# Memory attention and gates of the first layer spread over more projections; low weight parts taken from GpSimd to VectorE

## The chip, the cores and the metric

The kernel runs on one core of a Trainium2 chip. The core has five engines with a queue each, which meet only at semaphores: TensorE (PE; PEld is its weight load), VectorE (DVE), ScalarE (ACT), GpSimd (POOL) and SyncE (SP), which here only issues DMAs. The metric is the device time of one execution in microseconds (us), the median of several runs. A page and a trace of one profiled execution stand beside it.

## The reference, cut to what matters

The program is a two-layer trunk over 512 tokens of width 1024. The first layer mixes with an mLSTM (four heads of 256, chunk-wise) and a cross-attention to 256 memory tokens; the second layer uses latent attention and the same kind of memory attention. What the change touches is in the first layer:

```python
h = rmsnorm(x, norm_g)
qk, v, o, z, i_pre, f_pre, mq, mz = split_cols(h @ w_in, ...)
qk = silu(causal_conv(qk, conv_w, conv_b))            # 4 taps
...
lfc = log_sigmoid(f_pre); b = cumsum(lfc)             # gates: running sums and maxima
ht  = mlstm_chunkwise(q, k, v, i_pre, f_pre)
...
q  = rmsnorm(mq, q_gain)                              # memory attention, 4 heads of 128
p  = softmax(q @ mk.T * 128 ** -0.5)
y_mem = (p @ mv) * silu(mz)
return x + concatenate([y_m, y_mem]) @ w_out
```

All of it is float32 in and out.

## The kernel before, in words

Every float32 operand of a product is kept as two parts: a high part (`wh` of a weight, `hTh` of the activations), which ScalarE makes by a copy to a narrower format, and a low part (`wl`, `hTl`), the rest, which a subtraction makes (`split`, lines 130 and 131). A product is then three passes on TensorE: high by high, low by high (both line 162) and high by low (line 167). A weight block of 128 x 1024 numbers is loaded by SyncE into `wr` (two buffers), split into `wh` and `wl` (two buffers each) by `load`, and used in 24 matmuls. PSUM results are `acc` (four banks), `att` (two banks, attention) and `tp` (two banks, transposes).

The stages of the first layer in order: `mem_kv` and `x_prep`; `mem_proj`, which makes the memory queries and their gate and, by the way, the eight gate columns of the mLSTM; `gates`; then `a_qk(0)`, `a_v(0)`, `a_oz(0)`, the projections for the first mLSTM head, with `mem_attn` woven between them; then the other heads. `weave(main, side, plan)` takes a step of `main`, then as many steps of `side` as the plan has for it. `a_qk(0)` has 12 steps, three for each of its four weight blocks (24 matmuls each, then a convolution on VectorE, lines 611 to 616, in the one buffer `kl`). `mem_attn` has six steps: step i transposes the softmax of head i-1 (line 364), makes the scores of head i (two `att` tiles of 12 matmuls in all, a softmax on VectorE and ScalarE, lines 324 to 337) and the values of head i-2 (line 342 is their gate). `gates` computes on ScalarE and VectorE over 4 x 512 and 128 x 512 numbers, sends four rows of `m4` by a GpSimd DMA (line 584), and ends with two groups of transposes on TensorE (lines 589 and 594) that make `bcol` and `em`; `a_attn(0)`, the first mLSTM attention, is the first to read these.

The source's order isn't the final order. A scheduler that reckons with modelled times lines up each engine's instructions; each engine then runs its line strictly in order and waits where an operand or a buffer is not there.

`on_pool` is an iterator of 17 flags. `load` takes one flag for each weight block, and where it is true, the low part is made by GpSimd. The first nine blocks (those of `mem_proj`) are false, the next eight (four of `a_qk(0)`, four of `a_v(0)`) are true, and after them VectorE makes all.

Of the kernel before, what the change touches and what calls it, by code (L numbers as in the profile page):

```python
# [8 lines left out]
F32 = mybir.dt.float32  # L9
# [4 lines left out]
ALU = mybir.AluOpType  # L14
AX = mybir.AxisListType

P = 128
S = 512
# [22 lines left out]
def weave(main, side, plan=()):  # L41
    for i, _ in enumerate(main):
        for _ in range(plan[i] if i < len(plan) else 1):
            next(side, None)
    for _ in side:
        pass


def chain(*gens):
    for g in gens:  # L50
        yield from g


def drain(g):
    for _ in g:
        pass
# [3 lines left out]
def trunk(ctx: ExitStack, tc: tile.TileContext, pv_d, pos_d, x_d, memT_d, wmem_d, wg_d, wa_d, woa_d,  # L60
          wkva_d, wql_d, wb_d, wkvb_d, wqup_d, wob_d, out_d):
    nc = tc.nc
    V, A, G, PE = nc.vector, nc.scalar, nc.gpsimd, nc.tensor
# [17 lines left out]
    def st(shape, tag, bufs=1, dt=F32):  # L81
        return POOLS.get(tag, sp).tile(shape, dt, tag=tag, bufs=bufs, name=nm(tag))
# [9 lines left out]
    def s2(shape=(P, 512)):  # L92
        return st(list(shape), "s2", NS2)
# [7 lines left out]
    def tps(shape=(P, 512)):  # L101
        return pp.tile(list(shape), F32, tag="tp", bufs=2, name=nm("tp"))
# [22 lines left out]
        return pv[:, o:o + 1]  # L125


    def split(hi, lo, src, scale=None, eng=V):
        if scale is None:
            A.activation(hi, src, AF.Copy)  # L130
            eng.tensor_tensor(out=lo, in0=src, in1=hi.bitcast(F32), op=ALU.subtract)  # L131
        else:
            A.activation(hi, src, AF.Identity, scale=scale)  # L133
            V.scalar_tensor_tensor(out=lo, in0=src, scalar=scale, in1=hi.bitcast(F32),
                                   op0=ALU.mult, op1=ALU.subtract)

    on_pool = iter(())

    def load(src, nk, ncol, gain=None, pieces=1, raw=None):
        n = nk * ncol  # L140
        if raw is None:
            raw = wp.tile([P, 1024], F32, tag="wr", bufs=2, name=nm("wr"))
            nc.sync.dma_start(raw[:, :n], src)
        hi = wp.tile([P, 1024], F32R, tag="wh", bufs=2, name=nm("wh"))
        lo = wp.tile([P, 1024], F32R, tag="wl", bufs=2, name=nm("wl"))
        r3 = raw[:, :n].rearrange("p (k c) -> p k c", k=nk)
        if gain is not None:
            G.tensor_tensor(out=r3, in0=r3, in1=gain.unsqueeze(2).broadcast_to([P, nk, ncol]), op=ALU.mult)  # L148
        for i in range(pieces):
            ps_ = slice(i * n // pieces, (i + 1) * n // pieces)  # L150
            split(hi[:, ps_], lo[:, ps_], raw[:, ps_], eng=G if next(on_pool, False) else V)
        return (hi[:, :n].rearrange("p (k c) -> p k c", k=nk), lo[:, :n].rearrange("p (k c) -> p k c", k=nk))

    def prod(items, start, stop):
# [317 lines left out]
    def new_mkv():  # L472
# [4 lines left out]
                    in1=pv[:, _PV["mkg"]:_PV["mkg"] + 2], op=ALU.mult)  # L477
# [11 lines left out]
    mkT, mv = new_mkv()  # L489
    hT = (st([P, KT, S], "hTh", 1, F32R), st([P, KT, S], "hTl", 1, F32R))  # L490
    yT = (st([P, 12, S], "yTh", 1, F32R), st([P, 12, S], "yTl", 1, F32R))
# [55 lines left out]
    def gates():  # L547
        ps = tps([36, S])
        for t in range(NT):
            PE.transpose(ps[:, t * P:(t + 1) * P], gtk[:, t], ident)  # L550
        gw = st([36, 2, S], "s4", 2)
        fr = gw[32:36, 0]
        e = gw[32:36, 1]
        A.activation(fr, ps[32:36], AF.Identity, bias=pv[32:36, _PV["gb"]:_PV["gb"] + 1])
        A.activation(e, fr, AF.Abs)
        A.activation(e, e, AF.Exp, scale=-1.0)
        A.activation(e, e, AF.Ln, bias=one[32:36])
        lf = s2([4, S])
        V.scalar_tensor_tensor(out=lf, in0=fr, scalar=0.0, in1=e, op0=ALU.min, op1=ALU.subtract)
        ir = s2([4, S])  # L560
        A.activation(ir, ps[0:4], AF.Identity, bias=pv[0:4, _PV["gb"]:_PV["gb"] + 1])
        mask = s2([4, S])
        V.memset(mask, 1.0)
        V.memset(mask.rearrange("p (a b) -> p a b", a=NT)[:, :, 0:1], 0.0)
        b = s2([4, S])
        V.tensor_tensor_scan(b, mask, lf, 0.0, op0=ALU.mult, op1=ALU.add)
        R = s2([P, S])
        V.memset(R, 0.0)
        V.tensor_tensor(out=R[0:4], in0=ir, in1=b, op=ALU.subtract)
        b3 = b.rearrange("p (a b) -> p a b", a=NT)  # L570
        T = tiny([4, 3, 4])
        V.tensor_copy(T[:, 0], b3[:, :, P - 1])
        V.tensor_tensor(out=T[:, 1, 0:3], in0=T[:, 0, 0:3], in1=T[:, 0, 1:4], op=ALU.add)
        V.tensor_tensor(out=T[:, 2, 0:2], in0=T[:, 1, 0:2], in1=T[:, 0, 2:4], op=ALU.add)
        V.memset(mask, 0.0)
        V.tensor_copy(mask.rearrange("p (a b) -> p a b", a=NT)[:, 1:4, 0], T[:, 0, 0:3])
        V.tensor_tensor_scan(ir, mask, R[0:4], 0.0, op0=ALU.add, op1=ALU.max)
        R3 = R.rearrange("p (a b) -> p a b", a=NT)
        for k in range(1, 4):
            n = NT - k  # L580
            V.tensor_tensor(out=R3[32 * k:32 * k + 4, 0:n], in0=R3[0:4, 0:n],
                            in1=T[:, k - 1, 0:n].unsqueeze(2).broadcast_to([4, n, P]), op=ALU.add)
        for h in range(4):
            G.dma_start(m4[32 * h:32 * h + 1, :], ir[h:h + 1, :])
        V.scalar_tensor_tensor(out=lf, in0=b, scalar=-1.0, in1=ir, op0=ALU.mult, op1=ALU.subtract)
        V.tensor_scalar(lf, lf, 85.0, None, op0=ALU.min)
        tp = tps([P, NT, P])
        for c in range(NT):
            PE.transpose(tp[:, c], R[:, c * P:(c + 1) * P], ident)
        for k in range(4):  # L590
            V.tensor_copy(bcol[:, :, k], tp[:, :, 32 * k:32 * k + 4])
        tp = tps([P, NT, 4])
        for c in range(NT):
            PE.transpose(tp[:, c], lf[:, c * P:(c + 1) * P], ident[0:4, 0:4])
        A.activation(em, tp, AF.Exp)
# [3 lines left out]
    def a_qk(h):  # L599
        i0 = 4 + 20 * (h // 2) + 12 * (h % 2)  # L600
        r = 4 + 2 * (h % 2)
        for n, name in enumerate("qk"):
            heads[h][name] = st([P, 2, S], "qk", 4, F32R), yT[n][:, r:r + 2]
        for i in range(4):
            w = load(wa_d[i0 + i], KT, P)
            ps = acc()
            yield from proj_T(w, hT, ps)
            j = (8 if i >= 2 else 0) + 2 * h + i % 2
            tmp = st([P, 2, S], "kl")
            raw, u = tmp[:, 0], tmp[:, 1]  # L610
            A.activation(raw, ps, AF.Copy)
            V.tensor_scalar(u, raw, col("cw", 48 + j), col("cb", j), op0=ALU.mult, op1=ALU.add)
            for d in range(1, 4):
                V.scalar_tensor_tensor(out=u[:, d:], in0=raw[:, :S - d], scalar=col("cw", (3 - d) * 16 + j),  # L614
                                       in1=u[:, d:], op0=ALU.mult, op1=ALU.add)
            silu2(u, u, raw)
            hi, lo = heads[h]["qk"[i // 2]]
            split(hi[:, i % 2], lo[:, i % 2], u)
            yield
# [7 lines left out]
    def a_v(pr):  # L627
        vs = []
        for j in range(2):
            v = wide("v", 2, F32R), st([P, NT, 256], "u4", 5, F32R)  # L630
            G.memset(v[0][:, :, 256:258].bitcast(F32), 1.0)
            heads[2 * pr + j]["v"] = v
            vs.append(v)

        def evac(t, ps):
            for j in range(2):
                split(vs[j][0][:, t, 0:256], vs[j][1][:, t], ps[:, j * 256:(j + 1) * 256])

        yield from tok_proj(8 + 20 * pr, evac)

    def a_oz(h):
        gt = st([P, NT, 256], ("gt", "z4")[h % 2])
        heads[h]["g"] = gt

        def evac(t, ps):
            th = s2()
            A.activation(th, ps, AF.Tanh, scale=0.5)
            V.scalar_tensor_tensor(out=th[:, 256:], in0=th[:, 256:], scalar=1.0, in1=ps[:, 256:],
                                   op0=ALU.add, op1=ALU.mult)
            V.scalar_tensor_tensor(out=gt[:, t], in0=th[:, :256], scalar=1.0, in1=th[:, 256:],  # L650
                                   op0=ALU.add, op1=ALU.mult)

        yield from tok_proj(4 + 20 * (h // 2) + (8, 16)[h % 2], evac)
# [75 lines left out]
           (256, [(wa_d[c], 4 * c, 4) for c in range(2)])]  # L729
    wa_d = wa_d[2:]  # L730
    mu = []
    on_pool = iter((False,) * 9 + (True,) * 8)
    drain(mem_proj(wqa, wa_d, hT, None, (("u4", 5), ("qk", 4)), mu, gate_cols))
    gates()
    weave(chain(a_qk(0), a_v(0), a_oz(0)), mem_attn(mu, mkT, mv, yT), (1, 0) * 6)
    weave(chain(a_qk(1), a_oz(1)), a_attn(0))
    rope_tables()
    weave(chain(a_qk(2), a_v(1), a_oz(2)), a_attn(1))
# [11 lines left out]
    op = out_proj(woa_d, yT, a_done)  # L750
# [8 lines left out]
    mT, _ = load_memT(False)  # L759
# [377 lines left out]
```

## Time and profile before

| what | value |
|---|---|
| median of 3 runs | 787.78 us (786.49 to 788.13) |
| the profiled execution | 786.21 us, its span 784.4 us |
| busy share of the span | PE 97%, PEld 83%, DVE 64%, ACT 51%, POOL 26% |
| chain that ended last | PE 82%, DVE 11%, ACT 2%, POOL 1% |
| mean granted TensorE clock | 0.995 of full speed |

Read it so: TensorE is busy nearly all the time, and the chain of work that ended last is mostly TensorE. The span is 1.8 us shorter than the execution's own time, which has a launch and an end around it. The shares are means over very different stages, so the stretch that the change touches, some 82 to 156 us after the span's start, is looked at by itself.

### The profile page before, as it was taken

Reading aid. Unit: us, or ns where it says so; the run is one execution under the profiler, and the core shown is the slowest. Engines: PE = TensorE matmul, PEld = TensorE weight load, DVE = VectorE, ACT = ScalarE, POOL = GpSimd, SP = SyncE. Lnnn points to the kernel's source line nnn. Section 1 sums busy time; section 2 is a strip of 40 time slices with the busy share of each in tenths; the row PEclk is TensorE's granted clock in tenths of the full one; section 3 lists DMA queues with packets and bytes.
Section 4 is the critical chain, followed back from the end, with each engine's and each line's share of the span. In section 5 each row is a group of like instructions: output and inputs, shape, how many; then the busy total and the mean of one; then the engine's idle time right before and its main releaser. Section 6 shows DMA issues by size and latency. Waiting matters only on the chain.

```text
span 784.4 us, 11003 instructions
## 1 busy us (share of the span) xinstructions
PE 760.9 (97%) x3956; PEld 651.3 (83%) x3956; DVE 499.7 (64%) x970; ACT 400.7 (51%) x940; POOL 204.9 (26%) x294
## 2 busy tenths in 40 slices
PE   6999989999999999999999999999898999999997
PEld 5798877888888888888888888999787888888886
DVE  7753399837768836766434644586668787785432
ACT  4855645526455435536333647367656565644220
POOL 5311331201110101001001175250876361900000
PEclk9999999999999999999999999999999999999999
DMA  9322211223131223224444532211321111511141
GB/s 341 118 88 81 81 55 54 81 82 107 53 109 54 72 89 115 74 83 147 173 162 134 168 123 76 71 62 57 95 71 58 55 48 38 188 54 55 58 157 53
DMA packets 25190, 75.35 MB, mean 96 GB/s; under 512 B 2864, under 2 KB 3504, under 8 KB 25136
## 3 DMA queue, kind: packets, MB, share of 16 engines
q1 hardware_dynamic: 23568, 72.39, 27.6%
q10 hardware_dynamic: 1440, 2.25, 0.8%
q8 instruction: 31, 0.51, 0.3%
q14 instruction: 23, 0.19, 0.1%
q0 software_dynamic: 128, 0.01, 0.0%
HBM read 70.44 MB, written 4.19 MB: 95 GB/s over the span
## 4 chain that ended last, share of the span: by engine, by line
PE 82%; DVE 11%; ACT 2%; POOL 1%; issue 1%; DVEq 0%; ACTq 0%; POOLq 0%
PE acc L162 45%; PE acc L167 23%; PE att L162 3%; PE att L994 2%; PE att L167 2%; DVE wl L131 1%; PE tp L981 1%; DVE tiny L324 1%; PE tp L917 1%; DVE kl L614 1%; PE att L700 1%; PE att L701 1%; PE att L699 1%; ACT s L334 1%; POOL tiny L188 1%
## 5 line engine op out<-in xcount | busy, mean ns | idle before, releaser
L131 DVE TENSOR_TENSOR wl<-wr,wh 128x1024 fp32r<-128x1024 f32 (+5 forms) x109 | 130.3, 1195 | 152.6 <-ACT wh L130 131.2
L130 ACT ACTIVATE wh<-wr 128x1024 fp32r<-128x1024 f32 (+5 forms) x117 | 117.9, 1009 | 141.2 <-PE acc L162 114.3
L162 PE MATMUL acc<-wh,hTl 128*128 128x512 f32 (+4 forms) x352 | 123.6, 361 | 0.0
L162 PE MATMUL acc<-wh,hTh 128*128 128x512 f32 (+4 forms) x352 | 123.4, 363 | 0.2 <-ACT hTh L133 0.2
L162 PE MATMUL acc<-hTh,wh 128*128 128x512 f32 x256 | 102.4, 400 | 0.0
L162 PE MATMUL acc<-hTl,wh 128*128 128x512 f32 x256 | 101.1, 395 | 0.0
L167 PE MATMUL acc<-wl,hTh 128*128 128x512 f32 (+4 forms) x352 | 88.9, 359 | 0.0
L162 PE MATMUL acc<-wh,yTh 128*128 128x512 f32 x192 | 75.0, 394 | 0.0
L162 PE MATMUL acc<-wh,yTl 128*128 128x512 f32 x192 | 74.8, 390 | 0.0
L162 PEld LDWEIGHTS acc<-wh,hTh 128*128 128x128 f32 x352 | 65.2, 188 | 9.7 <-ACT hTh L133 0.7
L162 PEld LDWEIGHTS acc<-wh,hTl 128*128 128x128 f32 x352 | 65.5, 188 | 8.2
L167 PE MATMUL acc<-hTh,wl 128*128 128x512 f32 x256 | 69.7, 392 | 0.0
L167 PEld LDWEIGHTS acc<-wl,hTh 128*128 128x128 f32 x352 | 61.7, 188 | 8.8
L148 POOL TENSOR_TENSOR wr<-wr,pv 128x1024 f32<-128x1024 f32 (+2 forms) x24 | 42.7, 1783 | 88.9 <-DMA wr<-in_wb_dram 44.3
L162 PEld LDWEIGHTS acc<-hTl,wh 128*128 128x128 f32 x256 | 48.5, 190 | 9.2
L162 PEld LDWEIGHTS acc<-hTh,wh 128*128 128x128 f32 x256 | 48.6, 190 | 9.1
L167 PEld LDWEIGHTS acc<-hTh,wl 128*128 128x128 f32 x256 | 47.7, 188 | 9.8
L167 PE MATMUL acc<-wl,yTh 128*128 128x512 f32 x192 | 53.3, 389 | 0.0
L187 POOL TENSOR_SCALAR tiny<-tiny 128x2 f32<-128x2 f32 (+4 forms) x36 | 10.1, 280 | 165.1 <-ACT junk L192 52.3
L162 PE MATMUL acc<-wh,u 128*128 128x384 f32 (+1 forms) x160 | 39.0, 369 | 3.3 <-ACT junk L192 2.3
L167 PEld LDWEIGHTS acc<-wl,yTh 128*128 128x128 f32 x192 | 36.0, 188 | 7.4
L162 PEld LDWEIGHTS acc<-wh,yTh 128*128 128x128 f32 x192 | 36.1, 188 | 7.2
(286 smaller groups left out, 1496.7 us busy)
## 6 DMA issues: line engine op xcount, KB each, us to landing
wr<-in_wa_dram SPq DMA_DIRECT2D x46, 512.0 KB, 3.2
wr<-in_wb_dram SPq DMA_DIRECT2D x16, 512.0 KB, 3.5
wr<-in_woa_dram SPq DMA_DIRECT2D x12, 512.0 KB, 3.2
wr<-in_wob_dram SPq DMA_DIRECT2D x12, 512.0 KB, 3.2
wr<-in_wmem_dram SPq DMA_DIRECT2D x8, 512.0 KB, 3.4
yTh<-in_wmem_dram SPq DMA_DIRECT2D x6, 512.0 KB, 6.6
s<-in_memT_dram SPq DMA_DIRECT2D x8, 256.0 KB, 4.1
yTl<-in_x_dram SPq DMA_DIRECT2D x4, 512.0 KB, 9.0
```

Of the source, the lines that this page charges most:

```text
L130: A.activation(hi, src, AF.Copy)
L131: eng.tensor_tensor(out=lo, in0=src, in1=hi.bitcast(F32), op=ALU.subtract)
L148: G.tensor_tensor(out=r3, in0=r3, in1=gain.unsqueeze(2).broadcast_to([P, nk, ncol]), op=ALU.mult)
L162: PE.matmul(ps, x if lhs else w_[0], w_[0] if lhs else x, start=start and id(ps) not in seen, stop=False)
L167: PE.matmul(ps, a_[0] if lhs else w_[1], w_[1] if lhs else a_[0], start=False, stop=stop and left[id(ps)] == 0)
L187: G.tensor_scalar(t, ss, mul, add, op0=ALU.mult, op1=ALU.add)
L188: G.tensor_tensor(out=out, in0=t, in1=mhalf[:, :n], op=ALU.pow)
L324: V.tensor_reduce(mx[:, j:j + 1], ps, axis=AX.X, op=ALU.max)
L334: A.activation(out[j], ps, AF.Exp, bias=nb[:, j:j + 1], scale=rq[:, j:j + 1], accum_out=sm[:, j:j + 1])
L614: V.scalar_tensor_tensor(out=u[:, d:], in0=raw[:, :S - d], scalar=col("cw", (3 - d) * 16 + j), in1=u[:, d:], op0=ALU.mult, op1=ALU.add)
L699: PE.matmul(ps[:, :258], ph[:, blk(c, i)], v[0][:, c], start=c == 0, stop=False)
L994: PE.matmul(ps[:, i * P:(i + 1) * P], vt[:, c, h * P:(h + 1) * P], pTs[h][:, o:o + P], start=c == 0, stop=c == i)
```

## The change

Four edits. (1) `on_pool` is gone: all low weight parts are made by VectorE. (2) The plan of the first weave is `(1, 0, 0) * 6` in place of `(1, 0) * 6`: the six steps of `mem_attn` stand at the main steps 0, 3, 6, 9, 12 and 15 in place of 0, 2, 4, 6, 8 and 10, so the last two reach into `a_v(0)`. (3) `gates` is cut in two by a `yield`: its arithmetic stands where it did, and its transposes with what follows them come after the fourth step of `mem_attn`. (4) The gate arrays `R` and `lf`, which must now live longer, move from the shared `s2` buffers into the buffer `e`, which `a_attn(0)` uses later.

```diff
-    def split(hi, lo, src, scale=None, eng=V):
+    def split(hi, lo, src, scale=None):
         if scale is None:
             A.activation(hi, src, AF.Copy)
-            eng.tensor_tensor(out=lo, in0=src, in1=hi.bitcast(F32), op=ALU.subtract)
+            V.tensor_tensor(out=lo, in0=src, in1=hi.bitcast(F32), op=ALU.subtract)
...
-    on_pool = iter(())
...
-            split(hi[:, ps_], lo[:, ps_], raw[:, ps_], eng=G if next(on_pool, False) else V)
+            split(hi[:, ps_], lo[:, ps_], raw[:, ps_])
...
-        lf = s2([4, S])
+        keep = st([P, 1280], "e", 1)
+        R, lf = keep[:, 0:S], keep[0:4, S:2 * S]
...
-        R = s2([P, S])
...
         V.tensor_scalar(lf, lf, 85.0, None, op0=ALU.min)
+        yield
         tp = tps([P, NT, P])
...
-    on_pool = iter((False,) * 9 + (True,) * 8)
     drain(mem_proj(wqa, wa_d, hT, None, (("u4", 5), ("qk", 4)), mu, gate_cols))
-    gates()
-    weave(chain(a_qk(0), a_v(0), a_oz(0)), mem_attn(mu, mkT, mv, yT), (1, 0) * 6)
+    gc = gates()
+    next(gc)
+
+    def memory_and_gates():
+        for i, _ in enumerate(mem_attn(mu, mkT, mv, yT)):
+            if i == 3:
+                drain(gc)
+            yield
+
+    weave(chain(a_qk(0), a_v(0), a_oz(0)), memory_and_gates(), (1, 0, 0) * 6)
```

The orders of the two built programs are the same up to `mem_proj` (but for one memset of the buffer `e`, which goes to the very start) and from the last matmuls of `a_v(0)` on; SyncE's order is the same throughout. Between, they differ on four engines. In the changed kernel the line numbers from 137 on are one or two lower than before (326 becomes 324, 589 becomes 588).

GpSimd before, from the end of `mem_proj` to the broadcast of the first mLSTM attention (`wl` are low weight parts, `m_82` is `m4`):

```order
L188 TENSOR_TENSOR rq_472<-tiny_756,mhalf 128x16
L131 TENSOR_TENSOR wl_989<-wr_986,wh_988 128x1024
L131 TENSOR_TENSOR wl_1122<-wr_1119,wh_1121 128x1024
L131 TENSOR_TENSOR wl_1228<-wr_1225,wh_1227 128x1024
L584 DMA m_82_463<-s_163_943 1x16x32 x4
L131 TENSOR_TENSOR wl_1361<-wr_1358,wh_1360 128x1024
L131 TENSOR_TENSOR wl_1423<-wr_1420,wh_1422 128x1024
L131 TENSOR_TENSOR wl_1453<-wr_1450,wh_1452 128x1024
L631 MEMSET v_1410 128x4x2
L131 TENSOR_TENSOR wl_1483<-wr_1480,wh_1482 128x1024
L131 TENSOR_TENSOR wl_1513<-wr_1510,wh_1512 128x1024
L631 MEMSET v_1413 128x4x2
```

And GpSimd in the changed kernel, the same place:

```order
L186 TENSOR_TENSOR rq_472<-tiny_756,mhalf 128x16
L582 DMA m_82_463<-s_163_943 1x16x32 x4
L630 MEMSET v_1371 128x4x2
L630 MEMSET v_1374 128x4x2
L663 ISA
```

The eight subtractions are gone, and GpSimd has next to nothing left here. VectorE in the changed kernel, from the first gate instruction on (`e_941` holds `R` and `lf`; `tiny_996` are the maxima of the first softmax, `att_989` its scores):

```order
L558 SCALAR_TENSOR_TENSOR e_941<-s_161_936 4x512
L565 SCALAR_TENSOR_TENSOR s_165_948<-s_164_945,e_941 4x512
L567 TENSOR_TENSOR e_941<-s_163_943,s_165_948 4x512
L570 COPY tiny_952<-s_165_948 4x4
L573 MEMSET s_164_945 4x512
L322 TENSOR_REDUCE tiny_996<-att_989 128x1 x2
L131 TENSOR_TENSOR wl_1147<-wr_1144,wh_1146 128x1024
L571 TENSOR_TENSOR tiny_952<-tiny_952 4x3
L579 TENSOR_TENSOR e_941<-e_941,tiny_952 4x384
L611 TENSOR_SCALAR kl_1039<-kl_1039,pv 128x512
```

The third low weight part now stands among the gate's work; two more stand ahead of these rows and five behind them. TensorE before, where the gate's transposes stand (`tp_969` and `tp_978`) in the third block of `a_qk(0)`:

```order
L162 MATMUL acc_1231<-hTh_177,wh_1227 128x512
L589 MATMUL tp_969<-ident,s_166_950 128x128 x4
L162 MATMUL acc_1231<-hTl_178,wh_1227 128x512
L162 MATMUL acc_1231<-hTh_177,wh_1227 128x512
L162 MATMUL acc_1231<-hTl_178,wh_1227 128x512
L162 MATMUL acc_1231<-hTh_177,wh_1227 128x512
L162 MATMUL acc_1231<-hTl_178,wh_1227 128x512
L162 MATMUL acc_1231<-hTh_177,wh_1227 128x512
L162 MATMUL acc_1231<-hTl_178,wh_1227 128x512
L594 MATMUL tp_978<-ident,s_162_941 128x4 x4
```

TensorE in the changed kernel, where they stand now: behind the values of memory head 1 (`att_1323`) and ahead of those of head 2 (`att_1415`), in `a_v(0)`:

```order
L160 MATMUL att_1323<-z_208_1164,mv_175 128x512
L165 MATMUL att_1323<-s_207_1163,v_176 128x512 x2
L588 MATMUL tp_1334<-ident,e_941 128x128 x4
L593 MATMUL tp_1343<-ident,e_941 128x4 x4
L160 MATMUL att_1415<-s_228_1269,mv_175 128x512
L160 MATMUL att_1415<-gt_1270,mv_175 128x512
L160 MATMUL att_1415<-s_228_1269,mv_175 128x512
L160 MATMUL att_1415<-gt_1270,mv_175 128x512
L165 MATMUL att_1415<-s_228_1269,v_176 128x512 x2
L362 MATMUL tp_1401<-ident,s_235_1297 128x128 x2
```

They have moved back to behind the first blocks of `a_v(0)`, and the memory attention's last heads, which before lay in the second half of `a_qk(0)` and the start of `a_v(0)`, now lie in `a_v(0)` with few projection matmuls between them. VectorE's rows for this place in the changed kernel (`tiny_1295` and `tiny_1314` are the biases of the two softmaxes of head 3, `gt_1270` the low part of head 2's transposed softmax):

```order
L322 TENSOR_REDUCE tiny_1292<-att_1285 128x1 x2
L613 SCALAR_TENSOR_TENSOR kl_1240<-kl_1240,pv 128x510
L324 SCALAR_TENSOR_TENSOR tiny_1295<-tiny_1292,rq_472 128x2
L131 TENSOR_TENSOR yTl_180<-s_222_1224,yTh_179 128x512
L613 SCALAR_TENSOR_TENSOR kl_1240<-kl_1240,pv 128x509
L333 RECIPROCAL tiny_1298<-tiny_1298 128x2
L322 TENSOR_REDUCE tiny_1311<-att_1304 128x1
L335 TENSOR_SCALAR s_235_1297<-s_235_1297,tiny_1298 128x256 x2
L322 TENSOR_REDUCE tiny_1311<-att_1304 128x1
L131 TENSOR_TENSOR gt_1270<-tp_1271,s_228_1269 128x512
L131 TENSOR_TENSOR gt_1270<-tp_1278,s_228_1269 128x512
L324 SCALAR_TENSOR_TENSOR tiny_1314<-tiny_1311,rq_472 128x2
```

The rows of the last head's two softmaxes stand mixed with the third convolution of `a_qk(0)` (`kl_1240`), and the scores that they read (`att_1285`, `att_1304`) hold the two `att` banks until ScalarE has read them.

## Rows read from the trace of the kernel before

**Rows 1.** Windows: stretch; busy us (instructions) per engine; granted clock; DMA.
```profile
94.00:142.00 48.00, 43.48 (x216) 35.71 (x215) 45.77 (x101) 25.79 (x59) 12.54 (x10) 0.96 0.14 45
160.00:520.00 360.00, 360.00 (x1772) 305.09 (x1771) 213.19 (x383) 175.04 (x366) 66.08 (x86) 1.00 0.32 105
```

**Rows 2.** Waits of TensorE from 84 to 165: us, times, longest.
```profile
PE tp L594 <- DVE s L586: 2.3, 1, 2.3
PE att L162 <- ACT s L334: 1.8, 2, 1.4
PE tp L589 <- DVE s L581: 0.4, 1, 0.4
```

**Rows 3.** Windows around the fall of the granted clock.
```profile
109.60:111.40 1.80, 1.80 (x13) 1.68 (x14) 1.80 (x7) 0.86 (x3) 0.00 (x0) 1.00 0.83 282
111.50:114.80 3.30, 3.30 (x12) 2.61 (x10) 2.94 (x13) 2.81 (x8) 0.00 (x0) 0.50 0.04 10
```

**Rows 4.** Timeline of GpSimd, 80 to 150: start us, us, instruction [idle before].
```profile
82.14 2.41 POOL L131 TENSOR_TENSOR wl<-wr,wh 128x1024 fp32r<-128x1024 f32 x1 [11.95 <-ACT wh L130]
...
105.89 2.68 POOL L131 TENSOR_TENSOR wl<-wr,wh 128x1024 fp32r<-128x1024 f32 x1
...
141.87 5.33 POOL L131 TENSOR_TENSOR wl<-wr,wh 128x1024 fp32r<-128x1024 f32 x2 [10.29 <-ACT wh L130]
```

**Rows 5.** Timeline of VectorE, 60 to 165: long instructions.
```profile
96.66 1.75 DVE L572 COPY tiny<-s 4x4 f32<-4x4 f32 x1
...
106.25 2.33 DVE L326 SCALAR_TENSOR_TENSOR tiny<-tiny,rq 128x2 f32<-128x2 f32 x1
...
115.25 2.23 DVE L612 TENSOR_SCALAR kl<-kl,pv 128x512 f32<-128x512 f32 x1 [0.52 <-ACT kl L611]
...
124.91 2.48 DVE L131 TENSOR_TENSOR yTh<-kl,qk 128x512 fp32r<-128x512 f32 x1 [0.65 <-ACT qk L130]
...
141.40 3.55 DVE L614 SCALAR_TENSOR_TENSOR kl<-kl,pv 128x510 f32<-128x510 f32 x2
144.87 2.89 DVE L131 TENSOR_TENSOR yTl<-s,yTh 128x512 fp32r<-128x512 f32 x1
```

**Rows 6.** The same view: the same kinds of instruction at other moments.
```profile
100.15 0.15 DVE L576 COPY s<-tiny 4x3 f32<-4x3 f32 x1
100.22 0.53 DVE L612 TENSOR_SCALAR kl<-kl,pv 128x512 f32<-128x512 f32 x1
100.67 0.14 DVE L326 SCALAR_TENSOR_TENSOR tiny<-tiny,rq 128x2 f32<-128x2 f32 x1
...
112.65 0.69 DVE L131 TENSOR_TENSOR yTh<-kl,qk 128x512 fp32r<-128x512 f32 x1 [0.30 <-ACT qk L130]
...
130.29 1.52 DVE L614 SCALAR_TENSOR_TENSOR kl<-kl,pv 128x511 f32<-128x511 f32 x2
```

**Rows 7.** The same view: a weight's low part, a gated product, two ends of a stretch.
```profile
60.32 1.23 DVE L131 TENSOR_TENSOR wl<-wr,wh 128x1024 fp32r<-128x1024 f32 x1 [4.76 <-ACT wh L130]
...
82.58 0.69 DVE L206 SCALAR_TENSOR_TENSOR u<-s,acc 128x512 f32<-128x512 f32 x1 [3.20 <-ACT s L205]
...
93.60 0.68 DVE L559 SCALAR_TENSOR_TENSOR s<-s 4x512 f32<-4x512 f32 x1 [2.93 <-ACT s L557]
...
154.34 1.96 DVE L131 TENSOR_TENSOR u<-acc,v 128x256 fp32r<-128x256 f32 x5
```

**Rows 8.** Chain that ended last, 40 to 165: start us, us, what.
```profile
67.70 1.81 PE acc L162 x8
...
87.74 0.44 PE tp L314 x4
...
155.22 0.45 PE acc L167 x2
```

**Rows 9.** Timeline of ScalarE: gate input, one exponential of a softmax.
```profile
93.60 0.68 ACT L561 ACTIVATE s<-tp,pv 4x512 f32<-4x512 f32 x1
...
134.37 0.55 ACT L334 ACTIVATE s<-att,tiny,rq 128x256 f32<-128x256 f32 x1
```

## The prediction

> **What bounds the kernel now.** TensorE is busy for 97% of the span and makes most of the chain that ended last, so only what TensorE loses can be won. I read its waits in the stretch of the change first: three lines, 2.3, 1.8 and 0.4 us, 4.5 in all, and each names VectorE or a softmax behind it [rows 2]. Then the granted clock: behind the 2.3 us wait a stretch lies at 0.50, 1.2 of 2.4 GHz [rows 3]. The busy time of the longer stretch tells how long that lasted: its mean clock is 0.96 over 48 us [rows 1], 1.9 us lost at most; by the edges that I see between 111.4 and 114.8 it is 3.4 us at half speed, 1.7 us lost. So TensorE loses 4.5 + 1.7 = 6.2 us, and that is the most that the change can give here.
>
> Then who makes it wait. In those 48 us VectorE is busy for 45.77 [rows 1]; it is the bound of this stretch. But not all of that is work. Six instructions, two of them low parts of 128 x 512, take far longer than others of their kind [rows 5, 6]: 1.75 against 0.15, 2.33 against 0.14, 2.23 against 0.53, 2.48 against 0.69, 3.55 for two against 1.52, 2.89 against 0.69. The excess is 1.60 + 2.19 + 1.70 + 1.79 + 2.03 + 2.20 = 11.5 us. Each lies on a subtraction of GpSimd, of which there are eight in seven rows; the first, one from the middle and the last, a pair, are shown [rows 4]: the one of 105.89 ends at 108.57, the 0.14 us instruction that began at 106.25 ends at 108.58. Under the first, at 82.14, the gated product at 82.58 takes 0.69 as usual [rows 7]; it reads one operand in PSUM, the six stalled ones read only SBUF. So I take it that VectorE stands still while GpSimd subtracts. And the 2.3 us wait of TensorE is for a gate instruction that stood right behind the stall of 106.25.
>
> The Trainium skill says so as a rule (SBUF — State Buffer, "Who interferes with whom"): GpSimd and VectorE share a port pair under an exclusive lock, and a VectorE instruction with two SBUF inputs, or in a two-port mode, waits for the whole of a GpSimd one. By it all six stalls go with the eight instructions; the trace's ends agree, 108.57 and 108.58.
>
> **The change part by part.**
>
> *Low parts to VectorE.* It removes eight instructions from GpSimd, 2.4 to 2.7 us each, and adds eight to VectorE at 1.23 [rows 7]. Two of them stand ahead of the gates, where VectorE waits anyway (3.20 us idle ahead of one row [rows 7]), and cost nothing. Six lie in the stretch: 6 x 1.23 = 7.4 us. The stalls, 11.5, go. A low part now waits in VectorE's line in place of starting right behind ScalarE; TensorE needs it eight matmuls after the high part, and set against each other the two queues leave from 0.7 us up for each. That is cover, not gain; where VectorE slips by more than that, each microsecond is one of TensorE's.
>
> *Gates.* The gate chain starts later: its input transposes stand three matmuls further back, 3 x 0.23 = 0.7 us [rows 8], and on ScalarE an activation of 0.68 us [rows 9] now stands ahead of the rest of the chain: 1.4 us in all. So VectorE's first gate instruction comes at 95.0, not 93.60 [rows 7]. The transposes that made TensorE wait (2.3 and 0.4) stand over 20 us later, when their input is long there. Their readers, in the first mLSTM attention, come later still. GpSimd's DMA of `m4` has nothing ahead of it now; SyncE's order is the same, and its buffers come free at VectorE's pace. I price all of these at nothing.
>
> *VectorE's pace.* From the first gate instruction to the first low part of v (93.60 to 154.34 [rows 7]) it takes 60.7 us now. Then 60.7 - 11.5 + 7.4 = 56.6, from 95.0 to 151.6: 2.7 us earlier. That leaves out two memsets that move ahead of the stretch.
>
> *TensorE's pace.* The transposes ahead of `a_qk(0)` are through at 87.74 + 0.44 = 88.2, and `a_v(0)` ends at 155.22 + 0.45 = 155.7 [rows 8]; without its 6.2 us of losses that is 149.5. New waits have to be added. I set the two queues against each other at the place where the last memory heads stand close together in `a_v(0)`. TensorE reaches the values of head 1 after 138 matmuls of 512 columns at 1.81 / 8 = 0.226, 48 of 256 at half that, and 28 transposes at 0.11 [rows 8]: 31.2 + 5.4 + 3.1 = 39.7, at 127.9. They need the bank of the scores whose softmax bias (`tiny_1295`) is VectorE's 77th instruction from 95.0 on. Its mean, stalls taken off, is (45.77 - 7.3) / 101 = 0.38 [rows 1] (7.3 being the four stalls in that window): 73 x 0.38 + 4 x 1.23 = 32.7, at 127.7; with two exponentials of 0.55 [rows 9] 128.8. So TensorE waits 0.9 us. Six matmuls bring it to 130.2; the gate's transposes want a `tp` bank that VectorE frees eight instructions after the bias, at 130.7: 0.5. The values of head 2 want the next bank: bias two instructions on, 131.5, exponentials till 132.6, while TensorE is there at 131.3: 1.3. Together 2.7 us of new waits, and TensorE gains 6.2 - 2.7 = 3.5.
>
> The two paces give 2.7 and 3.5; I take 3.3, nearer to TensorE's, since the memsets are missing from the other. From 156 on both programs run in the same order and TensorE is busy for all of the 360 us from 160 to 520 [rows 1], so the gain stays. On the profiled execution: 786.21 - 3.3 = 782.9. The median is 787.78, 1.57 above it, and runs are compared by that: 787.78 - 3.3 = 784.5.
>
> **The rivals.**
>
> *A, new waits eat it.* The three new waits lie within 4 us. If they act as the old one of 2.3 us did, the clock falls once more and 1.7 us go [rows 3]; and if VectorE slips by one more microsecond, that comes on top. For it: VectorE has no idle left up to there. Against: the 1.4 us wait [rows 2] was followed by no fall, since one fall alone makes the mean of 0.96 [rows 1]. Gain 0.6 to 1.6: 786.2 to 787.2, 786.7 in the middle.
>
> The Trainium skill (TensorE: Matmul & The Clock Gate, "Part 1: The HAM clock gate") has the clock set by how busy the engine has been of late, so several short waits may count as one; no row here shows it.
>
> *B, no new waits.* VectorE runs with fewer gaps than its mean [rows 1], and all 6.2 us are won: 787.78 - 6.2 = 781.6. Against: VectorE would have to be faster than 151.6 by 2 us.
>
> *C, slower: VectorE takes the whole load.* The place is the same stretch. If the six long instructions are not held by GpSimd but by something that stays (their own operands, or fetching of instructions), VectorE has 60.7 + 7.4 = 68.1 us of work from 95.0 on and ends at 163.1, 8.7 later; TensorE, which was 1.3 us behind it, follows some 7 us later: 795. It decides as soon as more than a quarter of the 11.5 us stays (2.7 / 11.5). Against: six stalls on six subtractions, and equal ends.
>
> The Trainium skill has the advice that speaks for C (Perfetto Trace Analysis, "Optimizing Scalar/DVE Operations"): where VectorE is saturated, work may go to GpSimd, and this change takes it back; the same paragraph warns of the shared port, and the six long rows bear the warning out [rows 5].
>
> **How the numbers follow.** The forecast, 784.5 (783 to 786), has 0.63; A 0.19; B 0.11; C 0.07. What a measurement of this kernel can tell from no change is about 0.2%, 1.6 us: faster means below 786.2. The forecast's and B's cases are faster, but for 0.01: 0.73. A counts as the same but for its worst, 0.18 with that 0.01; slower is C and A's worst, 0.09. The range reaches from just past B to past the middle of A, 781.4 to 787.4, and leaves out C and the rest of A.
>
> **What would show it.** Right: no VectorE instruction of these kinds over 1 us in the stretch but the scans and low parts, GpSimd without a subtraction, TensorE's waits there under 3.5 us, none of them for the gate's last instruction, no stretch at half clock, and `a_v(0)` ending some 3 us earlier. Wrong: the long instructions stay (C); a new line in TensorE's waits for `wl` on VectorE, or the clock at 0.5 near 130 (A). A gain at 156 that isn't there at the end would refute that the later order carries it.

## The result, and the profile after

The changed kernel took 781.34 us (780.85 to 782.65, 4 runs) against 787.81 (786.49 to 788.13, 4 runs): a ratio of 0.9924 [0.9906, 0.9941], 6.5 us less. In a second comparison (e7 below) it took 783.41 (781.83 to 785.10, 6 runs) against 787.37: 0.9956 [0.9941, 0.997], 4.0 us less. The ten runs of both have a median of 782.4, and 56 runs of the kernel before, over all comparisons, one of 786.9. The forecast of 784.5 had the sign and the mechanism. The second median lies in the 783 to 786 of its main case; the first lies outside that, by 1.66, and just outside the whole range of 781.4 to 787.4, by 0.06. Which of 3.3, 4.0 and 6.5 is the change's own, the traces tell better than the times, as shown below: it is 4.6.

The windows of the changed kernel that answer to [rows 1] (stretch, then busy us and instructions of PE, PEld, DVE, ACT, POOL; granted clock; DMA):

```profile
94.00:142.00 48.00, 46.07 (x238) 38.44 (x238) 46.79 (x108) 28.52 (x62) 2.41 (x5) 1.00 0.15 48
160.00:520.00 360.00, 360.00 (x1777) 305.65 (x1776) 217.98 (x391) 178.50 (x375) 69.72 (x97) 1.00 0.32 104
```

In the same 48 us TensorE ran 238 matmuls in place of 216, the clock did not fall, GpSimd's 12.54 us became 2.41 (the DMA of `m4` and a memset), and VectorE is as busy as before, but now with work. TensorE's waits from 84 to 165 us, for [rows 2]:

```profile
PE att L160 <- ACT s L332: 1.5, 2, 0.8
PE tp L588 <- DVE gt L131: 0.4, 1, 0.4
```

4.5 us have become 1.94. Where they lie, by TensorE's timeline (start us, us, instruction, [idle before <- releaser]):

```profile
128.93 0.50 PE L160 MATMUL att<-s,mv 128*128 128x512 f32 x1 [0.69 <-ACT s L332]
...
131.00 0.63 PE L588 MATMUL tp<-ident,e 128*128 128x128 f32 x4 [0.41 <-DVE gt L131]
...
132.81 0.50 PE L160 MATMUL att<-s,mv 128*128 128x512 f32 x1 [0.84 <-ACT s L332]
```

These are the three places that the forecast named. VectorE's timeline for [rows 5, 7]: the gate's start, the instruction that took 1.75, a weight's low part and the row behind it, the two biases of the forecast, the first low part of v:

```profile
94.64 0.68 DVE L558 SCALAR_TENSOR_TENSOR e<-s 4x512 f32<-4x512 f32 x1 [2.93 <-ACT s L555]
...
97.20 0.15 DVE L570 COPY tiny<-s 4x4 f32<-4x4 f32 x1
...
98.42 1.20 DVE L131 TENSOR_TENSOR wl<-wr,wh 128x1024 fp32r<-128x1024 f32 x1
99.55 0.14 DVE L571 TENSOR_TENSOR tiny<-tiny 4x3 f32<-4x3 f32 x1
...
127.48 0.15 DVE L324 SCALAR_TENSOR_TENSOR tiny<-tiny,rq 128x2 f32<-128x2 f32 x1
...
131.36 0.15 DVE L324 SCALAR_TENSOR_TENSOR tiny<-tiny,rq 128x2 f32<-128x2 f32 x1
...
147.61 0.42 DVE L131 TENSOR_TENSOR u<-acc,v 128x256 fp32r<-128x256 f32 x1
```

No single instruction in the stretch takes over 1.23 us; the longest are the weights' low parts and the scans. The chain of waits (start us, us, what) puts the end of `a_v(0)` at 150.37 + 0.45, against 155.67 in [rows 8]:

```profile
150.37 0.45 PE acc L165 x2
```

**A length that the rest of the execution can't blur.** Executions of one kernel spread by 2 to 4 us, more than some parts of the change are worth. But the stretch that the change touches has two ends that are the same work in all these kernels: the transposes ahead of `a_qk(0)` (TensorE, line 314 before, 312 after) and a memset of `v` by GpSimd near 200 us. The kernel before, and then the changed one:

```profile
87.58 0.60 PE L314 MATMUL tp<-ident,s 128*128 128x128 f32 x4
...
202.12 0.11 POOL L631 MEMSET v<- 128x8 f32 x1 [19.98 <-PE att L700]
```

```profile
87.36 0.60 PE L312 MATMUL tp<-ident,s 128*128 128x128 f32 x4
...
197.29 0.11 POOL L630 MEMSET v<- 128x8 f32 x1 [19.67 <-PE att L699]
```

202.12 - 87.58 = 114.54 us before, and in two more profiles of that kernel (e9, e10) 114.54 and 114.49. After the change it is 197.29 - 87.36 = 109.93 us, and in e7 109.93 again. So the change takes 4.6 us off its own stretch. Every kernel below was measured by these two rows; but for the two kernels named, each has one profile. The third column is half of the time at half clock:

| kernel | stretch, us | lost to half clock within, us | ratio of the times |
|---|---|---|---|
| before (three profiles) | 114.54, 114.54, 114.49 | 1.7, 1.7, 0 | 1 |
| changed (two profiles) | 109.93, 109.93 | 0, 0 | 0.9924 and 0.9956 |
| e1 low parts alone | 111.24 | 0 | 0.9965 [0.9951, 0.9979] |
| e2 spread and split alone | 114.38 | 1.7 | 1.0 [0.999, 1.0011] |
| e11 split alone | 114.15 | 3.4 | 0.9998 [0.9987, 1.0009] |
| e6 all but the spread (the same program, see there) | 109.89 | 0 | 0.9947 [0.9935, 0.9959] |
| e5 spread wider | 111.53 | 1.7 | 0.9957 [0.9946, 0.9969] |
| e12 gates later, no spread | 110.71 | 0 | 0.9958 [0.9943, 0.9973] |
| e8 two low parts on GpSimd | 110.38 | 0 | 0.9963 [0.9948, 0.9978] |
| e4 dummy memsets | 112.13 | 0 | 0.9983 [0.9971, 0.9996] |
| e3 dummy subtractions | 117.47 | 1.7 | 1.0043 [1.0029, 1.0057] |

### The profile page after: what moved, and what is told of

It reads as the page before. It is cut to its first block, busy times and chain, and to the rows that moved or that the text cites. A ratio compares the mean times of both kernels' runs of the same rounds, so it can differ in the third digit from the quotient of the medians.

```text
span 779.1 us, 11004 instructions
## 1 busy us (share of the span) xinstructions
PE 760.0 (98%) x3956; PEld 651.6 (84%) x3956; DVE 497.6 (64%) x978; ACT 401.7 (52%) x940; POOL 185.1 (24%) x286
## 4 chain that ended last, share of the span: by engine, by line
PE 82%; DVE 11%; ACT 2%; issue 1%; POOL 1%; DVEq 0%; ACTq 0%; POOLq 0%
PE acc L160 45%; PE acc L165 23%; PE att L160 3%; PE att L1000 2%; PE att L165 2%; DVE wl L131 2%; PE tp L987 1%; DVE tiny L322 1%; DVE kl L613 1%; PE tp L923 1%; DVE s L335 1%; PE att L699 1%; PE att L700 1%; PE att L698 1%; DVE s L910 1%
## 5 line engine op out<-in xcount | busy, mean ns | idle before, releaser
L131 DVE TENSOR_TENSOR wl<-wr,wh 128x1024 fp32r<-128x1024 f32 (+5 forms) x117 | 140.5, 1202 | 156.8 <-ACT wh L130 132.6
```

The costliest lines, as they stand in the source:

```text
L131: V.tensor_tensor(out=lo, in0=src, in1=hi.bitcast(F32), op=ALU.subtract)
```

## The experiments

Theory L is the forecast's: GpSimd's subtractions hold VectorE, and TensorE waits for what is held.

**e1: the low parts alone**, in the kernel before:

```diff
-    on_pool = iter((False,) * 9 + (True,) * 8)
```

> The kernel before with one edit: all low weight parts on VectorE, the spread of the memory attention and the gates as before. Theory L (VectorE stands still while GpSimd subtracts, and that is what TensorE waited for): the six stalls, 11.5 us, are gone against 7.4 us of added subtractions; TensorE's 2.3 us wait for the last gate instruction falls below 0.5 and the half clock behind it goes, the 1.8 us for the softmaxes may stay: a gain of 3 to 5 us, 783 to 785. Rival S (the gain comes from the wider spread and the later gate transposes, VectorE being saturated either way): within 1.5 us of before, 786.3 to 789.

784.21 us against 786.58, 2.4 less, stretch 111.24. All long VectorE instructions are gone, the waits for the gate too, without the gate having been touched. TensorE's waits:

```profile
PE att L162 <- ACT s L334: 1.5, 2, 1.3
PE att L162 <- ACT s L130: 0.6, 1, 0.6
```

3.3 of the 4.6 us of the stretch come from this one line.

**e2: spread, split gates and the buffer `e`**, the eight low parts still on GpSimd (the changed kernel with the `on_pool` lines put back).

> The changed kernel, but the eight low parts go to GpSimd as before: the spread and the later gate transposes alone. Theory L: the stalls stay, some 11 us, so VectorE stays the bound; TensorE loses its wait for the gates but waits longer for the last memory heads: gain 0 to 2.5 us, 785.3 to 788. Rival S: most of the gain of 6.5 us, 781.5 to 783.5.

786.74 against 786.58: nothing. TensorE's waits:

```profile
PE tp L364 <- DVE s L337: 2.9, 1, 2.9
PE acc L162 <- ACT kl L612: 0.9, 1, 0.9
PE att L162 <- ACT s L334: 0.6, 1, 0.6
```

The 2.3 us wait for the gate is gone and 2.9 us for the first softmax have come in its place: another instruction stands behind the same stall, as VectorE's timeline shows.

```profile
105.88 2.29 DVE L326 SCALAR_TENSOR_TENSOR tiny<-tiny,rq 128x2 f32<-128x2 f32 x1
...
108.44 0.60 DVE L337 TENSOR_SCALAR s<-s,tiny 128x256 f32<-128x256 f32 x2
```

**e3: the stalls put back without the work.** The changed kernel, VectorE making all low parts, and GpSimd doing eight subtractions of the same size that nobody reads:

```diff
+        if next(on_pool, False):
+            spare = tabs.rearrange("p a b c -> p (a b c)")
+            G.tensor_tensor(out=spare, in0=hi.bitcast(F32), in1=hi.bitcast(F32), op=ALU.subtract)
```

> The changed kernel, and beside it GpSimd does eight subtractions of 128x1024 that nobody reads, released by the same high weight parts as the real ones were, into a table that is only written later; VectorE, TensorE, ScalarE and SyncE have the changed kernel's order, instruction for instruction. Theory L: at least five VectorE instructions that read SBUF alone take 1.5 to 2.5 us more, four of them ahead of 129 us, so TensorE's waits there grow from 1.9 by 5 to 7: 786 to 790. Rival S, or stalls with another cause: no VectorE instruction is longer and the time is the changed kernel's, 781 to 782.5.

790.27 against 786.58, slower than the kernel before and just above the 786 to 790 expected by Theory L; the stretch is 7.5 us longer than the changed kernel's, though the other engines' instructions and their order are the same. VectorE's timeline has the long rows again, on other instructions than before, and one of GpSimd's is long itself:

```profile
97.53 2.20 DVE L572 TENSOR_TENSOR e<-s,s 4x512 f32<-4x512 f32 x1
...
107.60 3.35 DVE L588 SCALAR_TENSOR_TENSOR e<-s,s 4x512 f32<-4x512 f32 x1
```

```profile
96.77 2.42 POOL L154 TENSOR_TENSOR tabs<-wh 128x1024 f32<-128x1024 f32 x1 [5.07 <-ACT wh L130]
...
115.00 4.09 POOL L154 TENSOR_TENSOR tabs<-wh 128x1024 f32<-128x1024 f32 x1 [4.60 <-ACT wh L130]
```

This is the case that rival C feared, VectorE with both the low parts and the stalls, though by another cause; against the kernel before it costs 3.7 us, half of C's 7. TensorE waits 4.0 us for `wl` here, the line that the forecast had named for the case that VectorE falls behind.

**e4: GpSimd busy, but reading next to nothing.** In place of each dummy subtraction one of two columns and two memsets of the whole buffer:

```diff
+            G.tensor_tensor(out=spare[:, :2], in0=hi[:, :2].bitcast(F32), in1=hi[:, :2].bitcast(F32), op=ALU.subtract)
+            G.memset(spare, 0.0)
+            G.memset(spare, 0.0)
```

> As the kernel with eight idle subtractions, but GpSimd only writes: a subtraction of two columns, then two memsets of 128x1024 in its place. The other four engines have the changed kernel's order. If VectorE is held only where both want the second read path, two-input instructions go on and at most some one-input ones (copy, tensor_scalar) are held: 781 to 783.5, fewer than three long instructions. If any GpSimd work holds it, as with the subtractions: 785 to 790.

785.62 against 786.58: the time is at the lower end of the second expectation, while the instructions behave nearly as the first one says. GpSimd works nearly as long for each block (the memsets take 0.95 us each), but the stretch is 2.2 us longer than the changed kernel's, not 7.5. VectorE's rows, and GpSimd's memsets under them:

```profile
96.82 0.68 DVE L574 TENSOR_TENSOR e<-s,s 4x512 f32<-4x512 f32 x1
...
107.85 1.37 DVE L342 TENSOR_SCALAR s<-s,tiny 128x256 f32<-128x256 f32 x2
109.15 1.25 DVE L591 TENSOR_SCALAR e<-e 4x512 f32<-4x512 f32 x1
...
111.71 1.18 DVE L342 TENSOR_SCALAR s<-s,tiny 128x256 f32<-128x256 f32 x2
```

```profile
96.84 0.95 POOL L155 MEMSET tabs<- 128x1024 f32 x1
...
108.03 1.05 POOL L155 MEMSET tabs<- 128x1024 f32 x1
109.14 0.98 POOL L156 MEMSET tabs<- 128x1024 f32 x1
...
111.52 0.98 POOL L156 MEMSET tabs<- 128x1024 f32 x1
```

So it isn't GpSimd's being busy that costs most, it is its reading beside VectorE's reading. The Trainium skill (SBUF — State Buffer, "Who interferes with whom") says the same: a VectorE instruction with two SBUF inputs contends with a GpSimd one that reads SBUF, not with one that only writes it. The trace agrees: the two-input subtraction at 96.82 takes its usual 0.68 us under a memset. The 2.2 us that remain are most likely the three `TENSOR_SCALAR` rows above, which have one full-size input: they take 1.37, 1.25 and 1.18 where the changed kernel has 0.60, 0.41 and 0.60, 2.2 us more in all, and each lies on a memset. No run tests that by itself.

**e7: the changed kernel again**, on the chip of e5, e6 and e8.

> The changed kernel once more, nothing edited, as the measure for the three beside it. Both theories: 5 to 6.5 us under the kernel before, 780 to 782, TensorE's waits from 84 to 165 us near 1.9 in three lines. If the gain comes out under 4 us, part of the 6.5 of the first comparison was the spread of single runs.

4.0 us less, and 783.41 lies outside the expected 780 to 782; the waits are the same to the tenth (1.5 and 0.4). So part of the first 6.5 was the spread of single runs. In this profile the clock fell at 8 and at 551 us, in the first one near 588, and in both at the very end; the ones at 8, 551 and 588 last 3.4 us each and so take up to 1.7. The mean granted clock of the first comparison's four runs was 0.995 to 0.998, that of these six 0.992 to 0.997, which points to luck of this kind.

**e6: the old density**, plan `(1, 0) * 6`, low parts on VectorE and split gates kept.

> The changed kernel with the memory attention at its old density, plan (1, 0) * 6; low parts on VectorE and the split gates stay. The first study of parts gave 2.4 us for the low parts alone and nothing for spread and split gates alone, so 2 to 3 us come only from both. Theory P (the spread gives them: the heads stand two steps apart and TensorE waits for softmaxes): 2 to 3 us slower than the changed kernel, waits for att on ScalarE's s from 1.5 us up. Rival G (the gates' later transposes give them): within 1 us of the changed kernel, TensorE's waits under 2.5 us.

783.14 against 787.37; the stretch 109.89, the waits 1.5 and 0.4. That is no wonder: in the two traces every engine runs the same instructions in the same order, all 3956 matmul records included. The scheduler makes the same order of both plans, so this is a third measurement of the changed kernel (4.2 us less). The spread, which names the change, does nothing here, and what closer heads would cost is not tested. Rival G's numbers hold: against e1 (111.24) the split gates give 1.35.

**e11: the split alone**, low parts on GpSimd, old density (e2 with `(1, 0) * 6`).

> The split gates and the buffer e alone: eight low parts on GpSimd, plan (1, 0) * 6. So far, by the stretch from the transposes ahead of a_qk(0) to the memset of v near 200 us, with the time lost at half clock taken off: before 112.7, low parts alone 111.1, split gates and spread without low parts 112.5, both 109.8, low parts and split gates without the spread 109.7. Theory L (while GpSimd holds VectorE, the split only moves the wait to another instruction): 112.2 to 112.9, the time within 1 us of before. Rival G (the split gates are worth their 1.4 us by themselves and the spread takes it back): 111.0 to 111.5, 1 to 2 us under before.

786.81 against 786.81, as Theory L has it, stretch 114.15; the 2.9 us wait of e2 is there again. The expected 112.2 to 112.9 had the half-clock time taken off; by that reckoning this profile, with 3.4 us lost, would give 110.7 and miss both theories' ranges. The reckoning was wrong (e10). By the stretch the split is worth 0.4 while the stalls are there, by the times nothing, and 1.35 once they are gone.

**e5: spread wider**, plan `(1, 0, 0, 0) * 6`.

> The changed kernel with the memory attention spread wider still, plan (1, 0, 0, 0) * 6. Theory L (GpSimd's subtractions held VectorE; what is left in the stretch are three short waits, 0.69, 0.41 and 0.84 us, where the last memory heads stand close together): with more projection matmuls between the heads these waits go, 1 to 1.9 us less than the changed kernel. Rival T (TensorE's path is already full and the last step of the memory attention, pushed further back, meets the output gate's projections): no change within 1 us of the changed kernel, new waits in place of the old.

783.94 against 787.37. Theory L's gain didn't come; the time is rival T's, within 1 us of the changed kernel, but without new waits. The three waits stay as they were (1.5 and 0.4): up to 142 us every engine's order is the changed kernel's. But the clock fell once, right behind them, without longer waits than the changed kernel has. The windows:

```profile
131.00:133.00 2.00, 1.00 (x9) 0.76 (x9) 2.00 (x8) 1.28 (x6) 0.00 (x0) 1.00 0.00 0
133.50:136.50 3.00, 3.00 (x11) 2.46 (x10) 2.64 (x6) 1.13 (x3) 0.00 (x0) 0.50 0.02 5
```

and the stretch is 111.53, 1.6 longer than the changed kernel's. That is the first half of rival A, seen: three short waits, and a fall at 133.5. It happened in one of the four profiles with these three waits (the changed kernel, e7, e6 and this).

**e8: two low parts on GpSimd**, the first two, `(False,) * 9 + (True,) * 2`.

> The changed kernel with the first two of the eight low parts on GpSimd again, those at 82 and 88 us, where VectorE has idle time and its instructions read one operand in PSUM or are small. Theory L (GpSimd holds only VectorE instructions that read SBUF alone): no long instruction on VectorE, the time within 0.8 us of the changed kernel. Rival W (any work on GpSimd costs TensorE time, by whatever way): 2 of 8 parts of the 9 us that eight dummy subtractions cost, 2 to 2.5 us slower than the changed kernel.

783.59, beside 783.41 of e7, as Theory L has it; stretch 110.38 against 109.93. The scheduler lines up TensorE a little differently here (waits of 1.3 and 0.6), so the 0.45 need not be GpSimd's. Under both subtractions, at 82.06 and 87.97, the gated product that reads PSUM takes its usual 0.69 us. The first:

```profile
82.50 0.69 DVE L206 SCALAR_TENSOR_TENSOR u<-s,acc 128x512 f32<-128x512 f32 x1 [3.21 <-ACT s L205]
```

**e12: the gates' transposes after the sixth step**, old density.

> Low parts on VectorE, plan (1, 0) * 6, and the gates' transposes after the sixth step of the memory attention in place of the fourth. It asks whether the three waits that are left (0.69, 0.41 and 0.84 us) hang on where the gates' transposes stand. Theory P (they take the tp banks that the last heads need, and set them): the 0.41 us go, and the stretch takes 109.3 us or less. Rival S (the two att waits come from two softmaxes with two att banks, whatever stands between): the two att waits stay, with up to 1 us more where the transposes no longer fill in, the stretch takes 109.4 to 110.8. The whole time by both within 1 us of the changed kernel, too little to tell; the stretch tells it.

782.84 against 786.81; stretch 110.71, both `att` waits still 1.5 together, and the 0.4 now falls on the softmax's transposes (line 362), which wait another 0.2 for a bias. Rival S: the waits that are left don't hang on the gates. It is 0.8 longer than e6, so the fourth step is the better place. No version tried beats the changed kernel clear of noise.

**e9 and e10: the kernel before, twice more**, unchanged, for its half clock.

> The kernel before once more, nothing edited, for a second profile of it. The question is the half clock at 111 us that the forecast counted as a loss of 1.7 us. Theory W (the clock falls there because TensorE waits 2.3 us just ahead): the fall is there again, between 110 and 116 us, and costs 1.7. Rival R (falls of 1.7 us come at changing places, two to three in an execution, and one lay there by chance): no fall between 100 and 120 us here or in the profile beside it. By both, the stretch from the transposes ahead of a_qk(0) to the memset of v near 202 us takes 112.7 us without such a fall.

> The kernel before a third time, for the same question. Theory W: a fall of the clock between 110 and 116 us, of 1.7 us, as in the other two. Rival R: none there, and as many falls in the whole execution as in the others, at other places.

787.42 and 787.25 us. In both the gate wait is 2.3 us again. In e9 the clock falls behind it, in e10 it does not. The two windows, e9's and then e10's:

```profile
110.20:113.20 3.00, 3.00 (x10) 2.52 (x10) 2.70 (x12) 1.84 (x5) 0.00 (x0) 0.50 0.21 85
```

```profile
111.50:114.80 3.30, 3.30 (x18) 2.73 (x18) 3.00 (x13) 2.14 (x8) 0.00 (x0) 1.00 0.14 55
```

So neither theory as put: the fall isn't bound to that wait (e10), but two of the three profiles have it there. And both were wrong in what they shared: without the fall the stretch is not 112.7 us, it is 114.49, as long as with it. Set TensorE's and VectorE's timelines of the two side by side. e10:

```profile
110.62 0.39 PE L162 MATMUL att<-mkT,u 128*128 128x256 f32 x1
...
119.06 0.40 PE L162 MATMUL acc<-hTl,wh 128*128 128x512 f32 x1
...
128.80 0.50 PE L162 MATMUL acc<-wh,hTh 128*128 128x512 f32 x1 [0.22 <-ACT kl L611]
130.55 0.66 PE L364 MATMUL tp<-ident,s 128*128 128x128 f32 x4 [0.17 <-DVE z L131]
...
131.97 0.39 PE L162 MATMUL acc<-wh,hTl 128*128 128x512 f32 x1
```

```profile
125.64 2.48 DVE L131 TENSOR_TENSOR yTh<-kl,qk 128x512 fp32r<-128x512 f32 x1 [0.65 <-ACT qk L130]
```

e9, the same instructions:

```profile
109.65 0.38 PE L162 MATMUL att<-mkT,u 128*128 128x256 f32 x1
...
119.64 0.40 PE L162 MATMUL acc<-hTl,wh 128*128 128x512 f32 x1
...
131.00 0.39 PE L162 MATMUL acc<-wh,hTl 128*128 128x512 f32 x1
```

```profile
124.67 2.49 DVE L131 TENSOR_TENSOR yTh<-kl,qk 128x512 fp32r<-128x512 f32 x1 [0.65 <-ACT qk L130]
```

e9 is 0.97 us ahead at its first row, falls behind by the half clock to 0.58 late at the second, and is 0.97 ahead again at the third. VectorE is 0.97 ahead all the way to 158 us, within 0.04, stalls included. TensorE at full clock gets further ahead and then stands: between 119 and 132 us its starts in e10 slip back by the same 1.55 us. Only three gaps there, 0.09, 0.22 and 0.17 us, are listed as idle; the rest is hidden by how the rows are drawn: a matmul of 0.39 us is usually followed by the next 0.23 later, so a start can come 0.16 late before any idle time is listed. At half clock these gaps are not there.

## Why the prediction was right, and where it wasn't

**The stalls: right.** Putting the subtractions back, with nobody reading them, brings long VectorE instructions and 7.5 us (e3); taking them away alone removes the waits for a gate that was not touched (e1). Of rival C nothing is left. The "equal ends" hold for the two shortest of the six; of the others, those of 115.25 and 124.91 end 0.27 and 0.54 us after GpSimd's (114.81 + 2.40 and 124.44 + 2.41), less than the 0.53 and 0.69 that they take unheld.

**What TensorE loses, 4.5 + 1.7 = 6.2: right in size, wrong in one of its two terms.** The step read the half clock as a loss beside the waits. e9 and e10 show that it costs nothing in the kernel before, because VectorE sets the pace there: without it the listed waits are 4.9 us in place of 4.5, and later starts that no row lists make up the rest. That 1.7 came close to these unlisted starts is luck. Where VectorE no longer sets the pace a fall does cost (e5, 1.6). I should have asked of the half clock what I asked of the waits: who is late if it goes?

**New waits, 0.9 + 0.5 + 1.3 = 2.7: right places, too large.** Measured 0.69 + 0.41 + 0.84 = 1.94. The two biases came at 127.48 and 131.36, forecast 127.7 and 131.5. TensorE's walk then gives 6.2 - 1.94 = 4.3, near the 4.6 of the stretch, where the forecast had 3.5.

**VectorE's pace, 151.6 for the first low part of v: the step that failed.** It came at 147.61. The step carried all of the 60.7 us over, VectorE's own idle time in it. The two windows, before from the first gate instruction to that low part, and after:

```profile
93.60:154.34 60.74, 56.22 (x274) 46.23 (x273) 56.82 (x110) 31.81 (x68) 17.85 (x12) 0.97 0.17 57
```

```profile
94.64:147.61 52.97, 51.04 (x261) 42.54 (x260) 50.49 (x113) 31.02 (x66) 2.52 (x6) 1.00 0.18 60
```

VectorE started at 94.64 and not at 95.0, its idle time fell from 3.9 to 2.5 us, and its busy time by 6.3, where my sum had 4.1. Three memsets that moved out of the stretch are 1.0 of the rest (I had named two of them and priced none). Of the remaining 1.2, half is the low parts' price: the one at 98.42 is drawn 1.20 long, but the next instruction starts 1.13 behind it, so that the six cost 6.8 and not 7.4. What is left is spread over many rows. Averaging this pace with TensorE's brought 3.5 down to 3.3; with the walk alone and the measured waits the forecast gain would have been 4.3.

**Which edit earns it: not foreseen.** Low parts 3.3, split gates 1.35 behind them, spread nothing, since with it and without it the program is the same (e1, e6). The forecast had put the end of the gate's waits down to the move of its transposes; the end of the stalls removes them by itself.

**The gain stays to the end: right.** The profiled executions differ by 4.83 us at the memset near 200 us (202.12 and 197.29) and by 5.36 as a whole (786.21 and 780.85). The rest of what the medians differ by is spread: ten runs of the changed kernel reach from 780.85 to 785.10.

**The rivals.** The first median lies next to rival B's 781.6, but its mechanism, no new waits, didn't come: all three are there. Rival A's fall of the clock came in one profile of four.

## What to carry to other kernels

An instruction that is many times as long as its kind is a wait in disguise: find what runs beside it on the other engines before moving any of the work that waits behind it, since moving that work alone may only give the wait another name (e2). Before a loss on the busiest engine goes into a sum, ask which engine sets the pace in that stretch; a loss beside a slower engine can be free (e9, e10). Before an edit is given credit, compare the built orders with it and without it: an edit of the source can leave the program as it was (e6). And where executions spread by more than a part is worth, measure that part between two rows that all versions share.

## What the runs showed of the hardware

The hold goes both ways. In e4 GpSimd's two-column subtraction takes 0.20 us when VectorE is at reductions, and 1.71 when it comes upon a low part and two more instructions that read only SBUF; the last of these ends at 107.92, the subtraction at 107.97:

```profile
106.26 1.71 POOL L154 TENSOR_TENSOR tabs<-wh 128x2 f32<-128x2 f32 x1
...
119.56 0.20 POOL L154 TENSOR_TENSOR tabs<-wh 128x2 f32<-128x2 f32 x1 [7.07 <-ACT wh L130]
```

```profile
105.98 1.21 DVE L131 TENSOR_TENSOR wl<-wr,wh 128x1024 fp32r<-128x1024 f32 x1
...
107.19 0.73 DVE L620 SCALAR_TENSOR_TENSOR kl<-kl,pv 128x509 f32<-128x509 f32 x1
```

The granted clock fell to half behind a 2.3 us wait in two of three profiles of one and the same program, and behind waits of 0.69, 0.41 and 0.84 in one of four; so where it falls is not fixed by the program, and a fall seen in a single profile is weak ground for a term of a sum.
